# ReLU and row sum: transfers of 16 rows with a two-pass bulk in place of 8 rows with fused rows

## The chip, the cores and the metric

The kernel runs on one core of a Trainium2 chip. The metric is the device time in microseconds of one execution. Ten runs of the kernel before gave a median of 164.6 us (164.5 to 164.82).

## The reference

`x` is a float32 array of 32 x 512 x 1024 standard normal numbers. The output is 32 x 512:

```python
relu_x = np.maximum(x, 0)
return np.sum(relu_x, axis=-1).astype(np.float32)
```

So 16,384 rows of 1,024 elements, 67.1 MB, are read once, negative elements count as zero, and each row gives one sum.

## The kernel before

The rows are dealt to the 128 partitions so that partition p holds rows 128p to 128p+127, which lie side by side in memory. A transfer brings some rows of every partition at once. The list `CHUNKS` gives how many: fifteen transfers of 8 rows (32 KB per partition, 4 MB in all), then 4, 2, 1 and 1 rows. Four buffers of 8 rows (`NB = 4`) are used in turn.

Three engines have a stream of instructions each, written out as three functions of a block:

- SP (SyncE) issues every load (L88). From the fifth load on it waits first until VectorE (L85) and ScalarE (L87) have finished with the buffer. At the end it waits for both engines (L93, L94), stores the sums from the tile `res` (L95) and waits for the store.
- VectorE waits for a load and takes the first rows of it, 52% rounded up: 4 of 8, 2 of 4, 1 of 2, and each single row. For each row one instruction (L107) takes the larger of the element and zero and adds up the row, with the sum written to one column of `res`.
- ScalarE waits for the same load and takes the other rows, one instruction for each (L134): Relu, with the sum given by the instruction's accumulator.

Each engine signals once per load, after its last row. The semaphores for loads are one per buffer. Both compute instructions write the rectified row back over the input, though nothing reads it. The order within each engine is the order in which the code was written; the only links between engines are the semaphores named above. When the block is left, the engines meet at a barrier (L38).

Of the kernel before, what the change touches and what calls it, by code (L numbers as in the profile page):

```python
# [1 line left out]

# [2 lines left out]

P = 128

CHUNKS = [8] * 15 + [4, 2, 1, 1]
NB = 4


def bass_relu_sum_kernel(
    nc: bass.Bass,
    x: bass.AP,
    out: bass.AP,
):
    fp32 = mybir.dt.float32
    ALU = mybir.AluOpType
    AF = mybir.ActivationFunctionType

    B, S, D = x.shape
    rows = B * S
    J = rows // P

    chunks = list(CHUNKS)
    assert sum(chunks) == J
    CHMAX = max(chunks)
    nchunks = len(chunks)
    assert nchunks >= NB

    xv = x.rearrange("b s d -> (b s) d").rearrange("(p j) d -> p j d", p=P)
    ov = out.rearrange("b s -> (b s)").rearrange("(p j) -> p j", p=P)

    def split_rows(nr):
        ndve = (nr * 52 + 51) // 100
        return ndve, nr - ndve

    with ExitStack() as ctx:  # L38
        buf = ctx.enter_context(nc.sbuf_tensor("buf", [P, NB, CHMAX, D], fp32))
        res = ctx.enter_context(nc.sbuf_tensor("res", [P, J], fp32))  # L40
        sem_in = [ctx.enter_context(nc.semaphore(f"sem_in{i}")) for i in range(NB)]
        sem_v = [ctx.enter_context(nc.semaphore(f"sem_v{i}")) for i in range(NB)]
        sem_a = [ctx.enter_context(nc.semaphore(f"sem_a{i}")) for i in range(NB)]
        sem_out = ctx.enter_context(nc.semaphore("sem_out"))
        block = ctx.enter_context(nc.Block("main_block"))

        fills = [0] * NB
        v_done = [0] * NB
        a_done = [0] * NB
        last_v = None  # L50
        last_a = None

        plan = []
        joff = 0
        for nr in chunks:
            b = fills[0] * 0 + (len(plan) % NB)
            k = fills[b]
            fills[b] += 1
            ndve, nact = split_rows(nr)
            d = dict(  # L60
                nr=nr,
                b=b,
                k=k,
                j=joff,
                ndve=ndve,
                nact=nact,
                wait_v=v_done[b],
                wait_a=a_done[b],
            )
            if ndve > 0:  # L70
                v_done[b] += 1
                last_v = (b, v_done[b])
            if nact > 0:
                a_done[b] += 1
                last_a = (b, a_done[b])
            plan.append(d)
            joff += nr

        @block.sync
        def _(eng):  # L80
            for p_ in plan:
                b, k, nr, j = p_["b"], p_["k"], p_["nr"], p_["j"]
                if k > 0:
                    if p_["wait_v"] > 0:
                        eng.wait_ge(sem_v[b], p_["wait_v"])  # L85
                    if p_["wait_a"] > 0:
                        eng.wait_ge(sem_a[b], p_["wait_a"])  # L87
                eng.dma_start(  # L88
                    out=buf[:, b, :nr, :], in_=xv[:, j : j + nr, :]
                ).then_inc(sem_in[b], 16)  # L90

            assert last_v is not None and last_a is not None
            eng.wait_ge(sem_v[last_v[0]], last_v[1])  # L93
            eng.wait_ge(sem_a[last_a[0]], last_a[1])  # L94
            eng.dma_start(out=ov[:, :], in_=res[:, :]).then_inc(sem_out, 16)  # L95
            eng.wait_ge(sem_out, 16)

        @block.vector
        def _(vec):
            for p_ in plan:  # L100
                b, k, nr, j, ndve = p_["b"], p_["k"], p_["nr"], p_["j"], p_["ndve"]
                if ndve == 0:
                    continue
                vec.wait_ge(sem_in[b], 16 * (k + 1))
                ins = None
                for r in range(ndve):
                    ins = vec.tensor_scalar(  # L107
                        out=buf[:, b, r, :],
                        in0=buf[:, b, r, :],
                        scalar1=0.0,  # L110
                        scalar2=None,
                        op0=ALU.max,
                        op1=ALU.add,
                        accum_out=res[:, j + r : j + r + 1],
                    )
                ins.then_inc(sem_v[b], 1)

        @block.scalar
        def _(act):
            for p_ in plan:  # L120
                b, k, nr, j, ndve, nact = (
                    p_["b"],
                    p_["k"],
                    p_["nr"],
                    p_["j"],
                    p_["ndve"],
                    p_["nact"],
                )
                if nact == 0:
                    continue  # L130
                act.wait_ge(sem_in[b], 16 * (k + 1))
                ins = None
                for r in range(ndve, nr):
                    ins = act.activation(  # L134
                        buf[:, b, r, :],
                        buf[:, b, r, :],
                        AF.Relu,
                        accum_out=res[:, j + r : j + r + 1],
                    )
                ins.then_inc(sem_a[b], 1)  # L140


# [1 line left out]
_INS = ['x']  # L144
_OUTS = [((32, 512), 'float32')]


# [21 lines left out]
```

## Time and profile before

| what | value |
|---|---|
| median of ten runs | 164.6 us |
| profiled execution, its own time | 164.75 us |
| its span, first to last instruction | 162.9 us |
| VectorE busy | 75.7 us (46%), 130 instructions |
| ScalarE busy | 68.6 us (42%), 127 instructions |
| one fused row on VectorE (L107) | 1216 ns, 65 of them |
| one fused row on ScalarE (L134) | 1045 ns, 63 of them, each with an accumulator read of 187 ns |
| read from memory | 67.11 MB, 412 GB/s over the span |
| load of 8 rows, from issue to landing | 34.2 us |
| last load, from issue to landing | 5.2 us, issued at 154.53 us |

The span is shorter than the execution's time[...]. Busy times of an engine are the sum over its instructions. The page divides the span into 40 slices and gives the busy share of each engine in tenths, and for the DMA line the mean over the sixteen DMA engines of the core. The chain of work starts at the last instruction and goes back, at each step, to what released it.

### The profile page before, as it was taken

Reading aid. Unit: us, or ns where it says so; the run is one execution under the profiler, and the core shown is the slowest. Engines: PE = TensorE matmul, PEld = TensorE weight load, DVE = VectorE, ACT = ScalarE, POOL = GpSimd, SP = SyncE. Lnnn points to the kernel's source line nnn. Section 1 sums busy time; section 2 is a strip of 40 time slices with the busy share of each in tenths; the row PEclk is TensorE's granted clock in tenths of the full one; section 3 lists DMA queues with packets and bytes.
Section 4 is the critical chain, followed back from the end, with each engine's and each line's share of the span. In section 5 each row is a group of like instructions: output and inputs, shape, how many; then the busy total and the mean of one; then the engine's idle time right before and its main releaser. Section 6 shows DMA issues by size and latency. Waiting matters only on the chain.

```text
span 162.9 us, 321 instructions
## 1 busy us (share of the span) xinstructions
DVE 75.7 (46%) x130; ACT 68.6 (42%) x127; POOL 0.2 (0%) x4
## 2 busy tenths in 40 slices
DVE  0006438092551907328092561907337091552995
ACT  3006337091551807227091551907336090542880
POOL 0000000000000000000000000000000000000000
DMA  5999999999999999999999999999999999999980
GB/s 193 442 418 451 426 426 450 410 426 459 410 442 442 418 451 426 430 426 418 442 434 410 442 442 418 442 434 426 434 426 434 442 418 442 434 410 410 412 349 19
DMA packets 2882, 67.19 MB, mean 412 GB/s; under 512 B 320, under 2 KB 448, under 8 KB 704
## 3 DMA queue, kind: packets, MB, share of 16 engines
q1 hardware_dynamic: 2880, 67.18, 96.3%
q14 instruction: 2, 0.02, 0.0%
HBM read 67.11 MB, written 0.07 MB: 412 GB/s over the span
## 4 chain that ended last, share of the span: by engine, by line
DMA 85%; DVE 13%; SPq 0%; issue 0%; DVEq 0%
DMA buf<-in_x_dram 85%; DVE buf L107 13%; SPq L88 0%; DVEq L38 0%
## 5 line engine op out<-in xcount | busy, mean ns | idle before, releaser
L107 DVE TENSOR_SCALAR_CACHE_REDUCE buf<-buf 128x1024 f32<-128x1024 f32 x65 | 75.6, 1216 | 85.2 <-DMA buf<-in_x_dram 85.0
L134 ACT ACTIVATE buf<-buf 128x1024 f32<-128x1024 f32 x63 | 65.8, 1045 | 89.0 <-DMA buf<-in_x_dram 89.0
L134 ACT ACTIVATION_READ_ACCUMULATOR buf<-buf 128x1 f32 x63 | 11.8, 187 | 0.0
L107 DVE DVE_READ_ACCUMULATOR buf<-buf 128x1 f32 x65 | 5.4, 82 | 0.0
L134 ACT ACT_TABLE_LOAD x1 | 1.3, 1283 | 0.7 <-PEq L154 0.7
L154 POOL MEMSET const-bfloat16-1.0<- 128x1 bf16 x1 | 0.1, 103 | 0.0
L154 POOL MEMSET const-uint8-127<- 128x1 uint8 x1 | 0.1, 102 | 0.0
L154 POOL MEMSET const-float32-1.0<- 128x1 f32 x1 | 0.1, 100 | 0.0
L154 POOL MEMSET const-float32-0.0<- 128x1 f32 x1 | 0.1, 99 | 0.2 <-issue 0.2
## 6 DMA issues: line engine op xcount, KB each, us to landing
buf<-in_x_dram SPq DMA_DIRECT2D x15, 4096.0 KB, 34.2
buf<-in_x_dram SPq DMA_DIRECT2D x1, 2048.0 KB, 29.3
buf<-in_x_dram SPq DMA_DIRECT2D x1, 1024.0 KB, 22.1
buf<-in_x_dram SPq DMA_DIRECT2D x2, 512.0 KB, 9.4
out_dram<-res SPq DMA_DIRECT2D x1, 64.0 KB, 1.5
```

The costliest lines, as they stand in the source:

```text
L107: ins = vec.tensor_scalar(out=buf[:, b, r, :], in0=buf[:, b, r, :], scalar1=0.0, scalar2=None, op0=ALU.max, op1=ALU.add, accum_out=res[:, ...
L134: ins = act.activation(buf[:, b, r, :], buf[:, b, r, :], AF.Relu, accum_out=res[:, j + r : j + r + 1],)
L154: nc = _bacc.Bacc("TRN2", target_bir_lowering=False, num_devices=1)
```

## The change

Loads carry 16 rows (64 KB per partition, 8 MB in all) into three buffers. There are seven such loads, then loads of 8, 4, 2 and 1 rows, and the last row comes in two halves of 512 elements, the second into a tile of its own, `last`.

The first load is made of two: SP issues partitions 0 to 63, and ScalarE issues partitions 64 to 127 on its own queue ahead of its computing. The other loads are issued by SP.

The first six loads (`NTWO = 6`) are computed in two passes: ScalarE rectifies 4, 5 and 7 rows, one instruction each, and after each of them VectorE sums the same rows with one reduction that gives one sum per row. In the sixth load the steps are 3, 4 and 5 rows; VectorE takes two more rows and ScalarE two more with the fused instructions of before. The seventh load and the tail use the fused instructions, row by row in turn between the engines. Of the last row ScalarE rectifies and sums the first half into element 513 of `last`; VectorE then rectifies and sums the second half and that element together.

SP refills a buffer when VectorE's third reduction on it has been done. It stores the sums after VectorE's last instruction. There is no block: the instructions of all engines are written one after the other, and the barrier on leaving the block is gone.

```diff
-CHUNKS = [8] * 15 + [4, 2, 1, 1]
-NB = 4
+D = 1024
+BIG = 16
+NBIG = 7
+NTWO = 6
+NB = 3
+STEPS = [4, 5, 7]
+MIXED = [3, 4, 5]
+TAIL = [8, 4, 2, 1]
+LAST = [512, 512]
...
+    tb = NBIG % NB
+    for c in range(NBIG + 1):
+        if c >= NB:
+            sp.wait_ge(s_dve, 3 * (c - NB + 1))
+        if c == 0:
+            for q, h in ((sp, 0), (act, P // 2)):
+                q.dma_start(
+                    out=buf[h : h + P // 2, 0, :, :], in_=xv[h : h + P // 2, 0:BIG, :]
+                ).then_inc(s_in[0] if h == 0 else s_half, 16)
+        elif c < NBIG:
+            sp.dma_start(
+                out=buf[:, c % NB, :, :], in_=xv[:, c * BIG : (c + 1) * BIG, :]
+            ).then_inc(s_in[c], 16)
+    r = 0
+    tail = []
+    for i, n in enumerate(TAIL):
+        sp.dma_start(
+            out=buf[:, tb, r : r + n, :],
+            in_=xv[:, NBIG * BIG + r : NBIG * BIG + r + n, :],
+        ).then_inc(s_in[NBIG + i], 16)
+        tail.append((r, n, s_in[NBIG + i]))
+        r += n
+    sp.dma_start(
+        out=buf[:, tb, r, 0 : LAST[0]], in_=xv[:, J - 1, 0 : LAST[0]]
+    ).then_inc(s_in[-2], 16)
+    sp.dma_start(out=last[:, 0 : LAST[1]], in_=xv[:, J - 1, LAST[0] : D]).then_inc(
+        s_in[-1], 16
+    )
...
+    for c in range(NTWO):
+        b, steps = c % NB, STEPS if c < NTWO - 1 else MIXED
+        act.wait_ge(s_in[c], 16)
+        if c == 0:
+            act.wait_ge(s_half, 16)
+        if steps is MIXED:
+            dve.wait_ge(s_in[c], 16)
+            for i in (BIG - 4, BIG - 3):
+                on_dve(*row(c, i))
+        r = 0
+        for i, n in enumerate(steps):
+            t = buf[:, b, r : r + n, :]
+            act.activation(t, t, AF.Relu).then_inc(s_act, 1)
+            dve.wait_ge(s_act, 3 * c + i + 1)
+            dve.tensor_reduce(
+                out=res[:, c * BIG + r : c * BIG + r + n], in_=t, axis=X, op=ALU.add
+            ).then_inc(s_dve, 1)
+            r += n
+        if steps is MIXED:
+            for i in (BIG - 2, BIG - 1):
+                on_act(*row(c, i))
...
+    for c in range(NTWO, NBIG):
+        act.wait_ge(s_in[c], 16)
+        dve.wait_ge(s_in[c], 16)
+        for i in range(BIG):
+            (on_act if i % 2 else on_dve)(*row(c, i))
+    for r, n, s in tail:
+        if n > 1:
+            act.wait_ge(s, 16)
+        dve.wait_ge(s, 16)
+        for i in range(r, r + n):
+            f = on_act if (i - r) % 2 else on_dve
+            f(buf[:, tb, i, :], res[:, j0 + i : j0 + i + 1])
+
+    act.wait_ge(s_in[-2], 16)
+    on_act(buf[:, tb, BIG - 1, 0 : LAST[0]], last[:, LAST[1] : LAST[1] + 1]).then_inc(s_tact, 1)
+    dve.wait_ge(s_tact, 1)
+    dve.wait_ge(s_in[-1], 16)
+    on_dve(last[:, :], res[:, J - 1 : J]).then_inc(s_tdve, 1)
...
+    sp.wait_ge(s_tdve, 1)
+    sp.dma_start(out=ov[:, :], in_=res[:, :]).then_inc(s_out, 16)
+    sp.wait_ge(s_out, 16)
```

`on_dve` and `on_act` are the two fused instructions of the kernel before; `row(c, i)` gives row i of load c and its column of `res`.

## The prediction

> **What bounds the kernel now.** I read the page's busy shares and its strip of slices first, then the chain that ended last, then the windows by stage, then the waits of the issuing queue, and last the timeline of the final microseconds.
>
> ```profile
> DVE  0006438092551907328092561907337091552995
> ACT  3006337091551807227091551907336090542880
> DMA  5999999999999999999999999999999999999980
> q1 hardware_dynamic: 2880, 67.18, 96.3%
> ```
>
> Both compute engines are busy under half of the span; the transfer engines are full from the second slice to the last but one. The windows say the same in numbers: from 23.2 to 140.0 us the DMA share is 1.00 at 432 GB/s.
>
> ```profile
> 0.00:23.20 23.20, 4.69 (x9) 5.59 (x10) 0.20 (x4) 1.00 0.93 391
> 23.20:140.00 116.80, 55.72 (x96) 51.17 (x96) 0.00 (x0) 1.00 1.00 432
> 140.00:158.40 18.40, 12.83 (x22) 11.87 (x22) 0.00 (x0) 1.00 0.97 409
> ```
>
> (Columns: stretch, length, VectorE, ScalarE, GpSimd busy and count, clock, DMA share, GB/s.) The chain of work agrees:
>
> ```profile
> 1.15 21.99 DMA buf<-in_x_dram
> ...
> 105.97 34.15 DMA buf<-in_x_dram
> ...
> 144.82 13.67 DMA buf<-in_x_dram
> 158.49 0.02 issue
> 158.51 1.23 DVE buf L107 x2
> 159.74 0.00 issue
> 159.75 1.22 DVE buf L107
> ```
>
> The VectorE pieces earlier in that chain only release a buffer whose transfer then queues behind three others (34.2 us from issue to landing, 9.7 us of it its own), so they cost nothing. At the end a row is exposed: the last transfer is issued at 154.53 and lands 5.2 us later, at 159.73; 1.22 us of VectorE follow, then the store.
>
> ```profile
> 159.75 1.22 DVE L107 TENSOR_SCALAR_CACHE_REDUCE buf<-buf 128x1024 f32<-128x1024 f32 x1
> 160.89 0.08 DVE L107 DVE_READ_ACCUMULATOR buf<-buf 128x1 f32 x1
> 161.00 0.35 SPq L95 DMA_DIRECT2D out_dram<-res  x1
> ```
>
> So the time is: start of the stream (about 2.2 us: 9.07 MB arrive by 23.2 us, which take 21.0 us at 432 GB/s), 67.11 MB through sixteen engines, one row, the store and the end. The profiled execution took 164.75 us, span 162.9, so 1.85 us lie outside; the ten runs have a median of 164.6, 0.15 lower.
>
> [...]
>
> **The change part by part.**
>
> *Packets.* In the trace's packet records 4 KB took 159.5 ns, 8 KB 310, 16 KB 612, 32 KB 1213.5: 0.03676 ns per byte and 8.8 ns per packet. An engine now moves 15x8 packets of 32 KB and 4x8 small ones, 152. After: 8 of 64 KB for each of seven bulk pieces, 8 each for 8, 4, 2, 1 rows, 16 for the two half rows, 104. 48 x 8.8 = 0.42 us less, and five loads fewer, each with one 9 ns semaphore write per engine: 0.05. No packet of 64 KB is shown: if it is cut in two, there are 160 packets and it costs 0.07. I take -0.47, ends -0.5 and 0.
>
> *First transfer from two queues.* SP and ScalarE each issue 64 partitions at once. ScalarE's issue (0.37 us here for SP's) and its table load (1.28) hide under the wait of 11.45 us for data that is now longer. The first packets start, by engine, from 1.7 to 3.4 us after the span's start, [...] from 0 to -0.8, I take -0.3. What it could cost is the main rival below.
>
> *Refill.* Three buffers of 16 rows hold as much as six of eight. Landings come every 2 x 9.715 = 19.43 us (four pieces per 38.86 us in the chain), first at 23.16, where the second piece lands now. ScalarE rectifies 4, 5, 7 rows. [...] estimates 3.60, 4.45, 6.16, less the overlap of 0.09 each: 13.9 us. VectorE sums them: [...] the operation is not in the trace[...]. Estimates 4.42, 5.48, 7.62: 17.5 us, after the first ScalarE step, so VectorE is done 21.7 us after the landing. The refill is issued then, one full piece (17.2 us) ahead of an empty queue. Cost nothing; the cover is 17.2 us, and without it each microsecond of lateness would be one of empty engines. SP's new waits have only later loads behind them (the last of them all six tail loads, issued in about 2 us at 0.33 each, with the same cover). ScalarE's wait for both halves holds the whole of the computing behind it, but no transfer for 17 us. VectorE's waits for ScalarE's steps leave it idle 3.6 us a piece, which the 19.43 us allow only once the backlog below is counted.
>
> *Bulk to tail.* VectorE's 17.5 fits in 19.43; it ends a piece 2.3 us after the next one's landing, while ScalarE is still at that one's first step (3.6), so no backlog builds up. The sixth piece (12 rows in two passes, 4 fused) ends about 138.2, before the seventh lands at 139.7. Then 8 fused rows per engine take 9.2 of 9.7 us, 4 take 4.6 of 4.9, 2 take 2.3 of 2.5, one row 1.22 of about 1.28. VectorE is never the later one by more than 0.1.
>
> *Last row.* Last landing L. First half lands L-0.66 (eight packets of 2 KB, 84 ns each). ScalarE 512 elements: 0.61, accumulator read net 0.1, end about L+0.07; VectorE's wait for it ends at L+0.12[...]. L+0.81 replaces L+1.24 (159.73 to 160.97): -0.43. Ends: -0.6 if ScalarE is early, 0 if the hop between engines costs half a microsecond.
>
> *Flat program.* The block's exit goes. SP's own waits show 1.2 us at L38 for the store, after its issue ended at 161.35, so it lands at 162.55; the span ends at 162.9 (0.2 of it another wait at L38, for the barrier): -0.35, if the launch's own end doesn't wait on something else (then 0). The branch ahead of the first issue: -0.03.
>
> Sum: -0.47 - 0.30 - 0.43 - 0.35 - 0.03 = -1.58 on 164.75, that is 163.17; on the median's level 0.15 lower. I take **163.2 us**, own range 162.4 to 164.0.
>
> **Rivals.** *Two halves collide (slower).* Place: the first transfer. [...] 8 packets of 2.42 us per engine (estimate from 0.03676 ns per byte) at half rate, +19.3 us; engines apart by x gain 8x. With x of 0.2 to 1.3 us, as the first packets start now, +9 to +18. Later pieces can't give it back, as the stream is full to the end. Forecast 172 to 182, likeliest 178. It turns the sign once it exceeds 1.6 us, 8% of the full collision. [...]
>
> [...] From 1.19 ns per element a piece takes 19.5 us, and VectorE becomes the bound; at 1.20 the gain is gone, at 1.25 (20.6 a piece) it ends some 7 us late. 165 to 171, say 167. [...]
>
> *The change does little.* 64 KB are cut in two, the start is unchanged, and the removed exit barrier isn't in the measured time: only the last row's -0.43 and the branch's -0.03 stay: 164.2.
>
> **How the numbers follow.** Main case 0.52, collision 0.38, slow reduction 0.04, little 0.06. A measurement here can tell about 0.2% (0.33 us) from no change. Faster: 0.52 and half of the little case, 0.55. Same: 0.04 (the other half and a little of the main case's upper end). Slower: the collision and the slow reduction less a sliver, 0.41. The range must reach into the collision: from 162.4 up to 179, which leaves out about half of it, and a thin lower end.
>
> **What would show it.** Right: wait of ScalarE for the first landing ends near 23.1; landings 19.4 us apart; no packet wait between; VectorE reductions of 4.4, 5.5 and 7.6 us; store issued near 159.8; no barrier after the store's wait. Collision: first landing at 32 to 42 us with 200 to 300 GB/s in the first slices, the rest of the kernel merely shifted. Slow reduction: DMA slices below 9 in the second half and VectorE at nine tenths throughout. Little: packet count as for 32 KB, same first landing as the second piece's now.
>
> The prediction is wrong if the two halves can't run side by side, which no row of this profile tests.

## The result

The changed kernel takes 182.91 us (median of 8 runs, 182.61 to 183.18), the kernel before 164.66. The ratio is 1.1108, with a 95% interval of 1.1099 to 1.1118: 11% slower. The profiled execution took 182.61 us, its span 180.9.

The forecast was 163.2. The time lies above the range, and above the 172 to 182 us of the rival that describes what happened.

The strip of slices of the changed kernel, from its page; a slice is 4.5 us:

```profile
DVE  0000000000398999997998799897989999789895
ACT  0000000004999299809991799349961996089773
DMA  9999998969998899999998999999989999899993
GB/s 232 232 232 232 232 203 174 203 145 435 464 464 377 377 406 464 464 464 464 420 406 348 449 464 464 464 464 406 406 348 464 464 464 464 348 420 402 427 391 113
q1 hardware_dynamic: 1952, 62.98, 86.5%
q10 hardware_dynamic: 80, 4.19, 10.8%
```

The DMA line stays high from the first slice to the last but one, nearly as before. The line under it tells the two parts of the span apart: about half the bytes per microsecond in the first nine slices, then the rate of before. A busy share doesn't show that: the windows below have the DMA share at 0.99 for 223 GB/s and for 429 alike. The two queues are SP's (q1) and ScalarE's (q10), whose 4.19 MB are the upper half of the first load.

The windows by stage (columns as in the prediction):

```profile
0.00:42.40 42.40, 0.00 (x0) 0.00 (x0) 0.20 (x4) 1.00 0.99 223
42.40:160.00 117.60, 103.66 (x25) 85.40 (x26) 0.00 (x0) 1.00 0.99 429
160.00:176.40 16.40, 15.53 (x29) 14.20 (x27) 0.00 (x0) 1.00 0.98 417
```

And the chain that ended last:

```profile
0.73 42.22 DMA buf<-in_x_dram
42.95 0.02 issue
42.97 0.02 ACTq L100
42.99 0.03 issue
43.02 1.28 ACT L108
44.31 0.01 issue
44.32 14.04 ACT buf L108 x3
```

The first load lands at 42.95 us; two loads of the kernel before, the same bytes, had landed at 23.1. From there on both stream at nearly the same rate. The excess at this point is 19.8 us, and the time is 18.3 us over the kernel before: the rest of the change gains about 1.5.

The packet records of the trace don't name the engines, but on each engine a packet begins where the one before it ended. The 128 packets of the two halves come in rounds of sixteen, one for each engine, and the rounds alternate strictly between the two queues. After each engine's first, a packet of 64 KB takes 4.86 to 4.90 us. From the third piece on, 64 KB take 2.42 us. Eight times the difference, 2.46 us, is 19.7 us. (In detail, against the kernel with one first transfer, below: the first packets of the engines lose 1.7 us on average, the other seven 2.46 each, and the first packets of the next load, which still take 3.0 us, 0.6 more.)

### The profile page after: what moved, and what is told of

It is laid out like the page before. It is cut to its first block, busy times and chain, and to the rows that moved or that the text cites. A ratio compares the mean times of both kernels' runs of the same rounds, so it can differ in the third digit from the quotient of the medians.

```text
span 180.9 us, 145 instructions
## 1 busy us (share of the span) xinstructions
DVE 121.8 (67%) x56; ACT 101.0 (56%) x55; POOL 0.2 (0%) x4
## 3 DMA queue, kind: packets, MB, share of 16 engines
q10 hardware_dynamic: 80, 4.19, 10.8%
## 4 chain that ended last, share of the span: by engine, by line
DMA 62%; ACT 24%; DVE 9%; another core or an unknown queue 2%; SPq 1%; issue 0%; ACTq 0%
DMA buf<-in_x_dram 62%; ACT buf L108 23%; DVE res L110 8%; SPq L71 1%; ACT L108 1%; ACT buf L86 0%; DVE last L89 0%; ACTq L100 0%
## 5 line engine op out<-in xcount | busy, mean ns | idle before, releaser
L110 DVE TENSOR_REDUCE res<-buf 128x4 f32<-128x4096 f32 (+3 forms) x18 | 100.3, 5602 | 54.6 <-ACT buf L108 54.6
L108 ACT ACTIVATE buf<-buf 128x4096 f32<-128x4096 f32 (+3 forms) x18 | 80.8, 4553 | 24.9 <-DMA buf<-in_x_dram 24.9
L86 ACT ACTIVATE buf<-buf 128x1024 f32<-128x1024 f32 (+1 forms) x18 | 18.4, 1021 | 9.7 <-DMA buf<-in_x_dram 9.7
L89 DVE TENSOR_SCALAR_CACHE_REDUCE buf<-buf 128x1024 f32<-128x1024 f32 x18 | 21.0, 1215 | 2.7 <-DMA buf<-in_x_dram 2.5
L86 ACT ACTIVATION_READ_ACCUMULATOR buf<-buf 128x1 f32 x18 | 3.4, 187 | 0.0
L89 DVE DVE_READ_ACCUMULATOR buf<-buf 128x1 f32 x18 | 1.5, 82 | 0.0
L89 DVE TENSOR_SCALAR_CACHE_REDUCE last<-last 128x513 f32<-128x513 f32 x1 | 0.7, 689 | 0.2 <-ACT buf L86 0.2
```

The lines of the kernel that those rows point to most:

```text
L86: return act.activation(t, t, AF.Relu, accum_out=acc)
L89: return dve.tensor_scalar(out=t, in0=t, scalar1=0.0, scalar2=None, op0=ALU.max, op1=ALU.add, accum_out=acc)
L108: act.activation(t, t, AF.Relu).then_inc(s_act, 1)
L110: dve.tensor_reduce(out=res[:, c * BIG + r : c * BIG + r + n], in_=t, axis=X, op=ALU.add).then_inc(s_dve, 1)
```

## The experiments

**One transfer again, and the cut by rows.** First, is the pair of halves the whole loss, and is it the two queues or the cut by partitions?

```diff
-            for q, h in ((sp, 0), (act, P // 2)):
-                q.dma_start(
-                    out=buf[h : h + P // 2, 0, :, :], in_=xv[h : h + P // 2, 0:BIG, :]
-                ).then_inc(s_in[0] if h == 0 else s_half, 16)
+            sp.dma_start(out=buf[:, 0, :, :], in_=xv[:, 0:BIG, :]).then_inc(s_in[0], 16)
```

(ScalarE's wait for `s_half` goes with it.)

> The first load is one transfer of 128 partitions from SP again; all else is as in the changed kernel. If the two halves are the whole loss (every theory below), the first landing is near 23.1 us instead of 43.0 and the time is that of the sum of the other parts, 163.2 us (162.6 to 164.0), 19.4 us or more under the changed kernel. If another part of the change also costs something, it stays above 164.6.

Measured: 163.14 us, ratio to the kernel before 0.9912 (0.9893 to 0.9931). The first landing is where the sum put it. From the waits of this kernel:

```profile
ACT buf L103 <- DMA buf<-in_x_dram: 48.1, 6, 21.1
DVE res L105 <- ACT buf L103: 35.3, 10, 26.7
```

(Columns: us in total, times, longest.) ScalarE's longest wait is 21.1 us, from the end of its table load at 2.0 to 23.1. So the halves are the whole loss, and everything else in the change together is a gain of 0.9%.

The second kernel keeps two queues, and cuts the first load by rows. (In the expectations, theory P has the rate go with the partitions that a transfer writes; Q, C and M are its rivals.)

```diff
-            for q, h in ((sp, 0), (act, P // 2)):
+            for q, h in ((sp, 0), (act, BIG // 2)):
                 q.dma_start(
-                    out=buf[h : h + P // 2, 0, :, :], in_=xv[h : h + P // 2, 0:BIG, :]
+                    out=buf[:, 0, h : h + BIG // 2, :], in_=xv[:, h : h + BIG // 2, :]
```

> The first load comes from two queues as in the changed kernel, but cut by rows: 128 partitions and 8 rows each. Theory P [...]: no collision, packets of 32 KB at 1.21 us, first landing near 23, 162.7 to 163.5 us. Rival Q (an engine that alternates between two queues moves each packet at half rate): packets at 2.4 us, first landing near 43, about 182 us.

Measured: 163.09 us, ratio 0.991 (0.9893 to 0.9926). From 11.8 to 21.5 us, while all engines alternate between the queues:

```profile
11.80:21.50 9.70, 0.00 (x0) 0.00 (x0) 0.00 (x0) 1.00 1.00 432
q10 hardware_dynamic: 144, 4.19, 6.0%
```

This is the full rate, with as many bytes on ScalarE's queue as in the changed kernel. Rival Q falls. The second queue also brings nothing: its time can't be told from that of one transfer.

**Both halves on one queue.** The reverse of that:

```diff
-            for q, h in ((sp, 0), (act, P // 2)):
+            for q, h in ((sp, 0), (sp, P // 2)):
```

> The same two halves of 64 partitions, both issued by SP on its one queue. Theory P: the lower half and then the upper half at about 220 GB/s, packets of 4.88 us, both landed near 43, 182 to 183 us (a little less, if the engines' start apart by about 1 us helps at the change of halves). Rival Q: packets of 2.42 us, landed near 23, 163.3 us.

Measured: 183.97 us, ratio 1.1183 (1.1166 to 1.12): still slow, by 1.1 us more than from two queues. Most packets take 5.11 to 5.13 us here, where 4.88 was expected; why, no run shows. One stretch of the lower half, and one that takes in the turn from the lower half to the upper:

```profile
2.10:11.80 9.70, 0.00 (x0) 0.00 (x0) 0.00 (x0) 1.00 0.98 203
21.50:31.20 9.70, 0.00 (x0) 0.00 (x0) 0.00 (x0) 1.00 1.04 216
```

**Which 64 partitions.** So far each half was at an edge, 0 to 63 or 64 to 127. Here 64 partitions across the middle, 32 to 95, come first, then the two edges of 32. No run before this one shows at what rate the middle runs.

```diff
-            for q, h in ((sp, 0), (act, P // 2)):
-                q.dma_start(
+            for lo, hi in ((32, 96), (0, 32), (96, 128)):
+                sp.dma_start(
-                    out=buf[h : h + P // 2, 0, :, :], in_=xv[h : h + P // 2, 0:BIG, :]
+                    out=buf[lo:hi, 0, :, :], in_=xv[lo:hi, 0:BIG, :]
-                ).then_inc(s_in[0] if h == 0 else s_half, 16)
+                ).then_inc(s_in[0] if lo == 32 else s_half, 16)
```

(ScalarE waits for 32 on `s_half`.)

> The first load in three transfers on SP's queue: partitions 32 to 95, then 0 to 31, then 96 to 127. Theory P: [...] 4 packets per engine run at 2.42 us (about 430 GB/s for 9.7 us), then 2 and 2 packets at 4.84 us; all landed near 33.3, 173.2 us. Rival C (any transfer of 64 partitions or fewer runs at half rate, whichever they are): as the changed kernel, landed near 43, 182.9 us. Rival Q: 163.3 us.

Measured: 174.47 us, ratio 1.0603 (1.0587 to 1.0619). The windows, each as long as half of the load's bytes take at full rate, show the step where it was expected:

```profile
2.10:11.80 9.70, 0.00 (x0) 0.00 (x0) 0.00 (x0) 1.00 1.07 432
11.80:21.50 9.70, 0.00 (x0) 0.00 (x0) 0.00 (x0) 1.00 1.02 216
21.50:31.20 9.70, 0.00 (x0) 0.00 (x0) 0.00 (x0) 1.00 1.04 216
```

64 partitions across the middle run at the full 432 GB/s; 0 to 31 and 96 to 127 at half, 216. Rival C falls: it isn't the number of partitions. The runs show the rate of each range of partitions; why the ranges differ, no run shows. Of the 1.3 us over 173.2, the packet records put about 0.55 in the slow packets (4.8 to 5.1 us on average by round, where 4.84 was expected), 0.4 in a later start of the first packets, and 0.5 in the first packets of the next load (2.9 us in place of 2.42).

**Where they are written, or where they are read?** One confusion was left. Partition p reads block p of the array, so the two halves of the partitions are also the two halves of the 67 MB, and partitions 32 to 95 read from both. Two kernels take the link apart. In the first each half of the partitions reads from the whole array:

```diff
-            for q, h in ((sp, 0), (act, P // 2)):
+            for q, h, o in ((sp, 0, 0), (act, P // 2, 1)):
                 q.dma_start(
-                    out=buf[h : h + P // 2, 0, :, :], in_=xv[h : h + P // 2, 0:BIG, :]
+                    out=buf[h : h + P // 2, 0, :, :], in_=xv[o:P:2, 0:BIG, :]
```

> As the changed kernel (two halves of 64 partitions from two queues), but partitions 0 to 63 take the rows of the even-numbered blocks of the source and partitions 64 to 127 those of the odd ones, so that each half reads from the whole of the array; the sums of this first load land in other places of the output than the reference has them. Theory P (the limit is where the halves are written[...]): no change, first landing near 43 us, 183 us. Rival M (the limit is where they are read: the lower half of the partitions is the first 32 MB of the array, the upper half the second): full rate, landing near 23, 163.3 us.

Measured: 183.32 us, ratio 1.1135 (1.1113 to 1.1158), with the first load landing late as before:

```profile
ACT L108 <- DMA buf<-in_x_dram: 43.7, 1, 43.7
```

In the second, partitions 32 to 95 read from the lower half alone:

```diff
-            for lo, hi in ((32, 96), (0, 32), (96, 128)):
+            for lo, hi, f in ((32, 96, 0), (0, 32, 64), (96, 128, 96)):
                 sp.dma_start(
-                    out=buf[lo:hi, 0, :, :], in_=xv[lo:hi, 0:BIG, :]
+                    out=buf[lo:hi, 0, :, :], in_=xv[f : f + hi - lo, 0:BIG, :]
```

> As the kernel with three first transfers (partitions 32 to 95, 0 to 31, 96 to 127), but partitions 32 to 95 take source blocks 0 to 63, and 0 to 31 take blocks 64 to 95, so the sums of the first load land in other places of the output. Theory P: as that kernel, 432 GB/s for the first 9.7 us and 174.5 us. Rival M: 216 GB/s from the start, since all of the first transfer's source lies in the first 32 MB, and about 184 us.

Measured: 174.53 us, ratio 1.0601 (1.058 to 1.0622), with the same step:

```profile
2.10:11.80 9.70, 0.00 (x0) 0.00 (x0) 0.00 (x0) 1.00 1.05 432
11.80:21.50 9.70, 0.00 (x0) 0.00 (x0) 0.00 (x0) 1.00 1.03 216
```

Neither time followed the source. Rival M falls; the limit goes with the partitions that are written.

**Do slow packets hold up only their own engines?** The prediction took it so: engines that are apart by x would gain 8x. In the changed kernel they are apart by up to 1.3 us and gain nothing: after each engine's first, no packet takes less than 4.86 us, where twice the 2.42 us of the full rate is 4.84. So a plain stream of 128 partitions, the kernel with one first transfer, was given a second load beside its first, of 64 KB to each of partitions 0 to 3. At the full 432 GB/s these 256 KB would take 0.6 us (an estimate). P1 and P2 both have the four packets share about the rate of one engine, which no run before this one shows. By P1 only the four engines that move them slow down, by P2 all sixteen.

```diff
+            act.dma_start(
+                out=buf[0:4, 2, :, :], in_=xv[0:4, 2 * BIG : 3 * BIG, :]
+            ).then_inc(s_half, 16)
...
+            if c == 2:
+                sp.wait_ge(s_half, 16)
```

> The first load is one transfer of 128 partitions from SP; beside it ScalarE's queue loads 64 KB to each of partitions 0 to 3 (rows that the third load brings again, which SP issues only after this)[...]. Theory P1 [...]: the other 12 engines go on at full rate, about 350 GB/s in the windows from 5 to 12 us, and the end moves by the 9.7 us that the crowded engines lose, to about 173 us. Theory P2 [...]: all of them fall to about a quarter while it lasts, 100 to 200 GB/s in those windows, with the same end or a little later. [...]

Measured: 171.28 us, ratio 1.0404 (1.0383 to 1.0425), 8.1 us over the kernel with one transfer, for 256 KB more. By the time alone P1 and P2 can't be told apart; the windows and the packets do that. The windows and the page's share of the second queue:

```profile
2.10:5.00 2.90, 0.00 (x0) 0.50 (x1) 0.00 (x0) 1.00 1.34 158
5.00:8.00 3.00, 0.00 (x0) 0.00 (x0) 0.00 (x0) 1.00 0.00 0
8.00:12.00 4.00, 0.00 (x0) 0.00 (x0) 0.00 (x0) 1.00 0.84 262
20.00:31.00 11.00, 0.00 (x0) 0.00 (x0) 0.00 (x0) 1.00 0.99 429
q10 hardware_dynamic: 8, 0.26, 1.3%
```

The empty stretch is one of booking: packets are booked where they begin, and none began there. The four packets to partitions 0 to 3 took 7.9 to 8.9 us, so that four engines together moved about as much as one does alone: 29 GB/s, against 27 for 64 KB in 2.42 us. The twelve packets of the other load that began beside them, on the other twelve engines, took 7.3 to 9.1 us; the first packets of the kernel with one transfer take 2.8 to 3.5. The packets that began from 5 to 12 us make 150 GB/s on average, where P1 expected 350. So P2 fits and P1 doesn't: beside the four packets to partitions 0 to 3, all sixteen engines took 7.3 to 9.1 us for a packet. That may be why being out of phase didn't help the halves; no run shows that it is. The end of the halves in the changed kernel fits too: the first packets of the next load, which has 128 partitions, took longer the earlier they began, 3.3 us for the first engine and 2.7 for the last. One control is missing: the same 256 KB to four partitions that are not neighbours. That a second queue alone does no such thing is shown by the cut by rows above. How the engines hold each other up isn't shown.

**The part alone, in the kernel before.**

```diff
+                if j == 0:
+                    eng.dma_start(
+                        out=buf[0:64, b, :nr, :], in_=xv[0:64, j : j + nr, :]
+                    ).then_inc(sem_h[0], 16)
+                    continue
...
+                if j == 0:
+                    act.dma_start(
+                        out=buf[64:128, b, :nr, :], in_=xv[64:128, j : j + nr, :]
+                    ).then_inc(sem_h[1], 16)
+                    act.wait_ge(sem_h[0], 16)
+                    act.wait_ge(sem_h[1], 16)
```

(VectorE and ScalarE wait for both halves; the later waits on this buffer count one load less.)

> The kernel before with this one part alone: its first load of 8 rows comes as two halves of 64 partitions from SP and ScalarE. Half the bytes of the changed kernel's first load, so half its loss: first landing at 23.2 to 23.7 instead of 13.46, 174.4 us (164.5 + 9.9). If the loss were a fixed cost of having two queues or of 64 KB packets: 164.5 or 184.

Measured: 174.29 us, ratio 1.0588 (1.057 to 1.0605). Half the bytes, half the loss, in packets of 32 KB:

```profile
2.10:11.80 9.70, 0.00 (x0) 0.00 (x0) 0.00 (x0) 1.00 1.07 233
11.80:21.50 9.70, 0.00 (x0) 0.00 (x0) 0.00 (x0) 1.00 0.97 216
34.00:140.00 106.00, 49.97 (x87) 45.79 (x87) 0.00 (x0) 1.00 1.00 432
```

**The terms of the gain.** With the halves out of the way, four more kernels, timed side by side, price the rest. The first has one first transfer again.

> The kernel with one first transfer of 128 partitions again, as the reference for the three that follow: 163.1 us (162.9 to 163.4), 1.4 us under the kernel before.

Measured: 162.95 us (162.85 to 163.07), ratio 0.9898 (0.9885 to 0.9912). This kernel is faster than both the kernel before and the changed one, by 1.0% and by 11%.

Each 16-row load as two of 8 rows:

```diff
-            sp.dma_start(
-                out=buf[:, c % NB, :, :], in_=xv[:, c * BIG : (c + 1) * BIG, :]
-            ).then_inc(s_in[c], 16)
+            for h in (0, 8):
+                sp.dma_start(
+                    out=buf[:, c % NB, h : h + 8, :],
+                    in_=xv[:, c * BIG + h : c * BIG + h + 8, :],
+                ).then_inc(s_in[c] if h == 0 else s_hi[c], 16)
```

(The first load likewise; the engines wait for both parts of each load.)

> As that kernel, with each 16-row load issued as two of 8 rows (packets of 32 KB; 56 more packets and 7 more semaphore writes on each engine). By the price per packet of the prediction (8.8 ns) it costs 0.55 us, 163.65. If the size of a packet doesn't matter at this end, 163.1.

Measured: 163.23 us (163.07 to 163.47): 0.28 more than the first of the four, and 0.4 more by the medians of the spans (161.85 against 161.45), where the price per packet gives 0.55. The times of the two kernels just touch, so this is a rough figure.

The last row whole:

```diff
-    on_dve(last[:, :], res[:, J - 1 : J]).then_inc(s_tdve, 1)
+    on_dve(buf[:, tb, BIG - 1, :], res[:, J - 1 : J]).then_inc(s_tdve, 1)
+    sp.wait_ge(s_tact, 1)
```

(The row comes in one load, ScalarE's half of it is gone, and SP waits for ScalarE's last row.)

> As that kernel, with the last row whole: one load, one fused instruction of VectorE, as in the kernel before. By the prediction's step the last instruction takes 1.24 us from the landing instead of 0.81, and eight packets fewer save 0.07: +0.35, 163.45. If the hand-over from ScalarE eats the gain: 163.1 or less.

Measured: 163.72 us (163.68 to 163.93): 0.77 more than the first of the four. By the medians of the spans it is 0.35 longer (161.8 against 161.45), which is what was expected. The sign is clear, the size in the measured time isn't: more than half of it lies outside the span, where nothing shows it.

The kernel before without its block:

```diff
-        block = ctx.enter_context(nc.Block("main_block"))
...
-        @block.sync
-        def _(eng):
+        def run_sync(eng):
```

(and so for the other two engines)

> The kernel before without its block, so without the barrier on leaving it; nothing else is changed. If the barrier is in the measured time as in the span: 164.55 - 0.35 = 164.2 us. If the launch's own end hides it: 164.5.

Measured: 163.85 us (163.7 to 164.1), ratio 0.9958 (0.9944 to 0.9971): 0.78 less, where the medians of the spans are 0.3 apart (162.5 against 162.8). The rest lies outside the span again. The waits of SP's queue, of the kernel before (first line) and of this one, show the barrier's wait gone:

```profile
SPq L38 <- PEq L38: 0.2, 1, 0.2
SPq L94 <- DMA out_dram<-res: 1.2, 1, 1.2
SPq L154 <- PEq L154: 0.7, 1, 0.7
```

## Why the prediction was wrong

**The choice between the cases.** The step that failed is the first transfer from two queues: it was put at -0.30 us, as a gain of the start that no trace shows, and it costs 19.8. The rival "two halves collide" had the place and the sign; it was given 0.38 and the main case 0.52. Every transfer of the kernel before has 128 partitions, so its trace gives no rate for 64, and both weights were the author's estimates. What spoke against the collision was only that a transfer of 64 partitions might go to eight engines, or that engines might fall out of step by a packet. The packet records show all sixteen engines on each half, and no two of them more than 1.3 us apart in a round. Two possibilities with no support in the trace should not have carried the main case.

**The size within the rival.** Its forecast was 178, from 19.3 us less 8 times the engines' distance in phase. The distance is there (up to 1.3 us) and brings nothing; 8 packets of 4.88 us cost 19.7. The step "engines apart by x gain 8x" is wrong: no packet after the first gained, and the load to partitions 0 to 3 above held up all engines. Without it, the rival would have given 163.2 + 0.3 + 19.7 = 183.2 against 182.91.

**Refill, bulk and tail were right.** The estimates for VectorE's reductions were 4.42, 5.48 and 7.62 us, for ScalarE's steps 3.60, 4.45 and 6.16. The trace of before, with rows of 1,024 elements alone and no such reduction, doesn't show them. The groups of the changed kernel:

```profile
L110 DVE TENSOR_REDUCE res<-buf 128x7 f32<-128x7168 f32 x5 | 38.1, 7620 | 2.7 <-ACT buf L108 2.7
L110 DVE TENSOR_REDUCE res<-buf 128x5 f32<-128x5120 f32 x6 | 32.9, 5484 | 0.0
L108 ACT ACTIVATE buf<-buf 128x7168 f32<-128x7168 f32 x5 | 30.8, 6159 | 0.0
L110 DVE TENSOR_REDUCE res<-buf 128x4 f32<-128x4096 f32 x6 | 26.5, 4416 | 51.9 <-ACT buf L108 51.9
L108 ACT ACTIVATE buf<-buf 128x4096 f32<-128x4096 f32 x6 | 21.7, 3614 | 19.6 <-DMA buf<-in_x_dram 19.6
```

So the estimates hold within 0.4%, and the rival of a slow reduction falls: it needs 1.19 ns an element, the longest reduction takes 1.06 (7620 ns for 7,168), and the stream stays at 429 GB/s.

**The sum without the collision came out, its terms less so.** It said 163.17; one transfer in place of the halves gives 163.14 and 162.95. That is in part luck, since 0.30 of the sum was the start from two queues, which these kernels don't have, and which gains nothing where it is free of the collision (163.09). Without it the sum is -1.28 us; against the kernel before, timed beside them, the two runs measure -1.38 and -1.68. Of its terms, the packets give about 0.3 to 0.4 (0.47 was taken), the missing block 0.78 of the time but 0.3 of the span (0.38 was taken, with the branch), and the halved last row 0.77 of the time but 0.35 of the span (0.43 was taken). The errors cancel in part. The end of the changed kernel shows the halved row at work:

```profile
177.85 0.63 ACT L86 ACTIVATE buf<-buf 128x512 f32<-128x512 f32 x1 [0.81 <-DMA buf<-in_x_dram]
178.60 0.69 DVE L89 TENSOR_SCALAR_CACHE_REDUCE last<-last 128x513 f32<-128x513 f32 x1 [0.20 <-ACT buf L86]
179.33 0.35 SPq L141 DMA_DIRECT2D out_dram<-res  x1
```

VectorE waits 0.20 us for ScalarE there and not for the transfer, as the prediction's step had it.

**A small miss.** ScalarE's table load was said to hide under its wait for data. In the changed kernel it runs after that wait, at 43.02 in the chain above: the wait for the second half is an instruction of its own ahead of the load, and holds it. It cost nothing that can be measured: the cut by rows has the same late load and takes 163.09 us. The refill's 17 us to spare would cover it. With one transfer there is no second wait, and the load runs at 0.72.

## What to carry to other kernels

A load should be cut along its rows, not into partitions 0 to 63 and 64 to 127: the first cut cost nothing here (163.09 us against 163.14 for one transfer), the second halved the rate for all bytes concerned (203 to 216 GB/s in the windows of one queue, 223 over the start from two, against 432). In a kernel that is bound by its stream, look at the bytes per microsecond of each stage, not at the busy share of the transfer engines, which stayed at nine tenths here while packets of 64 KB took 4.88 us instead of 2.42. Nothing of the loss at the start came back here: the first landing is 19.8 us late, and the end is still 19.8 us later than that of the kernel with one transfer.

## What was not expected of the hardware

Beside four packets of 64 KB to partitions 0 to 3, the twelve other engines were held up as well: their packets took 7.3 to 9.1 us instead of 2.8 to 3.5, and 256 KB of extra transfer cost 8.1 us. How isn't shown.

The two halves from one queue are slower than from two: mostly 5.11 us a packet against 4.88, 183.97 against 182.91 us. The cause is open.

Leaving out the block, with its exit barrier, was worth 0.78 us of the measured time, where the spans show 0.3.
